# Moving the residual stream and the norms of a two-layer decoder trunk from feature order to token order, under a scheduler that looks ahead

## The chip, the cores and the metric

The kernel runs on the 8 cores of one Trainium2 chip. Every core works through one sequence of the batch on its own, without talking to the others. The metric is device time in microseconds (us) of the slowest core. Engines are called PE (the tensor engine), ACT (scalar), DVE (vector), POOL (GpSimd) and SP (sync).

Executions fall in two states. In the slow one, a die's cores are granted a lower PE clock and the run is some per cent longer, whatever the kernel.

## The reference, cut to what matters

```python
def rms_norm(x, g):
    y = x * lax.rsqrt(jnp.mean(x * x, axis=-1, keepdims=True) + 1e-6)
    return y * g

for layer in range(2):            # x is (8, 4096, 1024) float32
    h = h + 0.5 * rms_norm(swiglu(rms_norm(h, g0), wg, wu, wd), g1)   # hidden width 2816
    h = h + rms_norm(mixer(rms_norm(h, g2)), g3)   # layer 0: RG-LRU, layer 1: window attention
    h = h + 0.5 * rms_norm(swiglu(rms_norm(h, g4), wg2, wu2, wd2), g5)
```

There are six sub-layers, each with a norm before it and a norm after it. The mean of squares runs over the 1024 features of a token.

## The kernel before

A core cuts its 4096 tokens into 8 tiles of 512. Two tiles ("chains" 0 and 1) are always in flight, so that PE can multiply for one while the other is in a norm. The whole program is recorded as a graph of operations. A small list scheduler with a model of durations then fixes the order of the instructions on each engine. PE's order is fixed: an instruction whose input is late holds up everything behind it. Weights (float32 in memory) stream through slots in on-chip memory, and a DMA that POOL issues casts them to bf16.

Before the change the residual X lies in feature order: 128 features on the partitions, 512 tokens along the free axis, 8 chunks. The sum over features therefore crosses partitions, and PE does it, by multiplying the squares with a matrix of ones:

```python
X = [sb(f"X{s}", [128, NCH, T], F32) for s in range(NS_)]      # feature order, NCH = 8, T = 512

def norm_stats(s, src, key):                 # sum of squares over partitions, on PE
    h = Ps(s)
    for lo, hi in ((0, 6), (6, 8)):
        mm(s, [h], group(h, [ONES[:, :]] * (hi - lo), [src[s][:, kc, :] for kc in range(lo, hi)], ...
    return h

def rstd(s, h, to_psum):                     # x ** -0.5 as exp(-0.5 * ln(x)): an ACT table load
    act(s, ... out=RT[s][:, :], in_=PS[h.bank], func=AF.Ln, bias=EPSC[:, 0:1], scale=1.0 / D ...)
    act(s, ... out=PS[h.bank], in_=RT[s][:, :], func=AF.Exp, scale=-0.5 ...)

def norm_in(s, gcol):                        # the norm in front of a sub-layer
    ...                                      # squares, unless norm_out has made them
    h = norm_stats(s, SQ, "SQ")
    rstd(s, h, True)
    for kc in range(NCH):                    # PE may go on after the last of these
        dve(s, ... scalar_tensor_tensor(out=XN[s][:, kc, :], in0=X[s][:, kc, :],
            scalar=PV[:, gcol + kc:gcol + kc + 1], in1=PS[h.bank], op0=ALU.mult, op1=ALU.mult) ...)

def norm_out(s, gt, gcol, presq, final=None):   # norm after it, and the residual
    h = norm_stats(s, SQ, "SQ")
    rstd(s, h, True)
    ...                                      # 8 x (multiply, multiply-add) on DVE, squares on ACT
```

In the scheduler, each chain offers only the first operation of its queue on an engine:

```python
for q in qs:
    if q:
        o = q[0]
        r = self.ready(o)
```

Attention begins, after its norm, with two large memsets on DVE, which will matter later:

```python
dve(s, lambda e: e.memset(QZ[64:128, :, 0, :], 0.0), [], rQZ, n=4096)
dve(s, lambda e: e.memset(QZ[0:64, :, 1, :], 0.0), [], rQZ, n=4096)
```

## Time and profile before

| | before |
|---|---|
| time, median of 3 runs | 5182.59 us (5176.87 to 6037.99) |
| profiled run, slowest core | 5150.3 us, PE clock 0.977 |
| PE busy | 4786.3 us, 93% |
| PE idle before and between its instructions (sum over the timeline) | 335 us |
| rest of the span (after the last matmul, and gaps too short to be listed) | 29 us |

From the page of the kernel before: the engines' busy time, three rows of the span in 40 slices (busy share in tenths; PEclk is the granted clock in tenths) and the two large DMA queues (packets, MB, share of time).

```profile
PE 4786.3 (93%) x23872; PEld 2238.6 (43%) x23872; DVE 1951.0 (38%) x3805; ACT 2540.8 (49%) x4635; POOL 805.9 (16%) x1488
PE   6989899998999898999999989899899998999868
PEclk9989999999999999999999999999999999999989
DMA  8979778996999885999689978699698997869927
q0 software_dynamic: 213120, 666.99, 81.3%
q1 hardware_dynamic: 18720, 33.74, 2.3%
```

PE is the limit, with holes, and the DMA row is not far below it: most slices stand at 8 or 9.

The groups of instructions that make the norm's sums and its root (busy us, mean ns | idle before them):

```profile
L316 PE MATMUL psall<-SQ,ONES 128*128 128x512 bf16 x720 | 192.7, 402 | 127.9 <-ACT SQ L440 80.8 <-ACT SQ L403 44.3 <-ACT SQ L529 2.1
L509 ACT ACT_TABLE_LOAD x127 | 162.9, 1283 | 104.9 <-PE psall L316 102.7 <-DVE XN L409 1.1
L391 ACT ACT_TABLE_LOAD x82 | 105.2, 1283 | 65.7 <-PE psall L316 65.0
```

The mean of 402 ns is the length of one matmul's record, and such records overlap. Back to back one takes 0.216 us (94 matmuls in 20.45 us at 1599.83 in PE's timeline).

What PE waits for (total us, times, longest):

```profile
PE psall L316 <- ACT SQ L440: 80.8, 8, 12.2
PE psall L316 <- ACT SQ L403: 44.3, 3, 34.8
PE psall L316 <- ACT ST L743: 40.5, 84, 0.6
PE psall L775 <- ACT FB L781: 36.0, 72, 0.5
PE psall L316 <- DVE XN L409: 29.6, 5, 7.2
PE psall L316 <- DMA W<-wgu: 25.4, 9, 5.4
PE psall L316 <- DVE HST L635: 25.4, 3, 8.5
```

Eight waits of up to 12 us stand for the squares of an input norm, and a few of 7 to 8.5 us follow them. One such place in PE's timeline (start, us, instruction, count, idle before it):

```profile
1772.07 2.08 PE L316 MATMUL psall<-SQ,ONES 128*128 128x512 bf16 x8
1786.34 3.50 PE L316 MATMUL psall<-SQ,ONES 128*128 128x512 bf16 x8 [12.19 <-ACT SQ L440]
1798.30 3.57 PE L316 MATMUL psall<-XN,W 128*128 128x512 bf16 x8 [8.47 <-DVE HST L635]
```

The first row sums the output norm, the second the next input norm. PE sits idle 12.2 us while residual and squares are made, and 8.5 us while root and multiplies are made. (The profile names HST L635 for the second wait because that small copy ended last on DVE, at 1798.17. The last of the eight multiplies that PE needs ended 0.1 us before it.) The other tile is in its recurrence and has nothing for PE.

The rows also show a second cost of such gaps. Eight ones-matmuls take 2.08 us before the gap and 3.50 us after it, because the granted clock has fallen:

```profile
1780.00:1790.00 10.00, 3.50 (x8) 1.02 (x8) 10.00 (x17) 5.82 (x11) 0.00 (x0) 0.52 0.38 77
```

(The columns are those of the next table; the clock is 0.52.) In this trace the clock stands at 0.5 in 24 stretches of 3.4 to 24 us. Worked out from these records, the PE work inside them took some 55 us longer than at full clock.

The last 300 us in windows of 50 us (PE busy; PEld; DVE; ACT; POOL; clock; DMA share; GB/s):

```profile
4900.00:4950.00 50.00, 35.96 (x321) 24.52 (x319) 35.54 (x116) 44.72 (x142) 2.64 (x5) 0.97 0.33 54
4950.00:5000.00 50.00, 31.51 (x217) 18.46 (x214) 20.89 (x65) 35.85 (x92) 2.11 (x4) 0.81 0.31 60
5000.00:5050.00 50.00, 40.57 (x168) 17.36 (x169) 14.84 (x23) 11.06 (x17) 4.75 (x9) 0.85 0.59 112
...
sum 300.00, PE 220.44 PEld 110.44 DVE 104.57 ACT 124.38 POOL 32.61; mean PE 36.74 PEld 18.41 DVE 17.43 ACT 20.73 POOL 5.43
```

One tile is left alone here, with its attention and its last FFN, and PE is busy 220 of 300 us. In the trace the last attentions of the two tiles begin 431 us apart (at 4489 and 4920).

### The profile page before, as it was taken

How to read it: one execution, taken by the hardware profiler on the slowest of the kernel's cores; microseconds unless marked ns; L12 is line 12 of the kernel's file. 1: busy time of each engine (PE TensorE's matmuls, PEld its weight loads, DVE VectorE, ACT ScalarE, POOL GpSimd, SP SyncE). 2: the span in 40 equal slices, each digit the busy share in tenths (PEclk: the TensorE clock that was granted, in tenths of full speed). 3: DMA queues.
4: the chain of work that ended last, by engine and by line, in shares of the span. 5: the costliest groups of instructions: out<-in, count | busy, mean ns of one | idle time of the engine just before them, and what ended most of it. 6: DMA issues, size and time to landing. Idle time of an engine off the chain costs nothing.

```text
span 5150.3 us, 71937 instructions; the slowest of 8 cores (5110.8 to 5150.3 us)
## 1 busy us (share of the span) xinstructions
PE 4786.3 (93%) x23872; PEld 2238.6 (43%) x23872; DVE 1951.0 (38%) x3805; ACT 2540.8 (49%) x4635; POOL 805.9 (16%) x1488
## 2 busy tenths in 40 slices
PE   6989899998999898999999989899899998999868
PEld 2434344444444344444444434444444443444333
DVE  1344353225352426324444343521534344432251
ACT  2466365227563637424565463732747365453261
POOL 1111111210121110121112111012111211111101
PEclk9989999999999999999999999999999999999989
DMA  8979778996999885999689978699698997869927
GB/s 135 151 113 146 120 119 154 148 161 110 153 149 155 126 134 100 176 147 148 126 135 166 153 119 146 110 152 158 105 172 135 162 146 125 137 113 147 154 54 119
DMA packets 232200, 705.33 MB, mean 137 GB/s; under 512 B 25760, under 2 KB 26016, under 8 KB 231840
## 3 DMA queue, kind: packets, MB, share of 16 engines
q0 software_dynamic: 213120, 666.99, 81.3%
q1 hardware_dynamic: 18720, 33.74, 2.3%
q8 instruction: 201, 3.29, 0.3%
q14 instruction: 159, 1.30, 0.1%
HBM read 1317.19 MB, written 33.55 MB: 262 GB/s over the span
## 4 chain that ended last, share of the span: by engine, by line
PE 81%; ACT 6%; DVE 4%; DMA 4%; issue 3%; SPq 0%; POOL 0%; DVEq 0%; ACTq 0%; POOLq 0%
PE psall L316 81%; DMA W<-wgu 4%; ACT FB L736 2%; DVE ST L727 1%; ACT FB L781 1%; DVE XN L409 1%; DVE FB L758 1%; DMA X<-xT 1%; DVE FB L419 1%; PE psall L775 0%; ACT ST L743 0%; DVE ST L751 0%; ACT L391 0%; ACT RT L391 0%; ACT psall L394 0%
## 5 line engine op out<-in xcount | busy, mean ns | idle before, releaser
L316 PE MATMUL psall<-XN,W 128*128 128x512 bf16 x12864 | 2836.5, 381 | 85.4 <-DVE XN L409 29.6
L316 PEld LDWEIGHTS psall<-XN,W 128*128 128x128 bf16 x12864 | 1261.2, 98 | 1620.0 <-issue 134.3
L511 DVE TENSOR_TENSOR BIG<-SG,psall 128x512 bf16<-128x512 bf16 x704 | 478.4, 686 | 2166.4 <-PE psall L316 2075.5
L316 PE MATMUL psall<-BIG,W 128*128 128x512 bf16 x5632 | 1223.6, 379 | 0.0
L509 ACT ACTIVATE SG<-psall 128x512 bf16<-128x512 f32 x704 | 418.9, 597 | 1118.8 <-PE psall L316 1047.6
L316 PEld LDWEIGHTS psall<-BIG,W 128*128 128x128 bf16 x5632 | 551.0, 98 | 664.5
L870 POOL DMA_DIRECT2D W<-wgu x704 | 385.8, 549 | 2481.9 <-PE psall L316 2127.4
L527 ACT ACTIVATE FB<-psall 128x512 f32<-128x512 f32 x256 | 152.3, 595 | 818.8 <-PE psall L316 818.8
L870 POOL DMA_DIRECT2D W<-wdn x512 | 270.2, 528 | 1212.4 <-PE psall L316 1174.3
L316 PE MATMUL psall<-SQ,ONES 128*128 128x512 bf16 x720 | 192.7, 402 | 127.9 <-ACT SQ L440 80.8
L419 DVE TENSOR_TENSOR FB<-FB,psall 128x512 f32<-128x512 f32 x320 | 215.1, 683 | 153.0 <-ACT psall L394 153.0
L440 ACT ACTIVATE SQ<-X 128x512 bf16<-128x512 f32 x320 | 200.7, 628 | 134.6 <-DVE X L435 129.6
L736 ACT ACTIVATE FB<-psall,ST 128x256 bf16<-128x256 f32 x512 | 260.6, 575 | 3.2 <-DVE ST L730 3.1
L409 DVE SCALAR_TENSOR_TENSOR XN<-X,PV,psall 128x512 bf16<-128x512 f32 x336 | 227.2, 742 | 87.9 <-ACT psall L394 87.8
L316 PE MATMUL psall<-HY,W 128*128 128x512 bf16 x1024 | 231.0, 387 | 5.1 <-DVE HY L638 4.4
L509 ACT ACT_TABLE_LOAD x127 | 162.9, 1283 | 104.9 <-PE psall L316 102.7
L727 DVE TENSOR_REDUCE ST<-psall 128x1 f32<-128x512 f32 x256 | 176.0, 688 | 71.7 <-PE psall L316 66.6
L870 POOL DMA_DIRECT2D W<-wmix x200 | 105.5, 528 | 603.0 <-PE psall L316 599.2
L625 DVE TENSOR_TENSOR FB<-FB 128x512 f32<-128x512 f32 x64 | 43.4, 690 | 344.3 <-ACT FB L621 344.0
L316 PE MATMUL psall<-BIG 128*128 128x256 bf16 x512 | 122.8, 272 | 51.4 <-ACT ST L743 40.5
L316 PEld LDWEIGHTS psall<-SQ,ONES 128*128 128x128 bf16 x720 | 71.5, 102 | 227.1 <-issue 153.9
L316 PEld LDWEIGHTS psall<-HY,W 128*128 128x128 bf16 x1024 | 102.0, 100 | 132.6 <-issue 17.0
(92 smaller groups left out, 3337.3 us busy)
## 6 DMA issues: line engine op xcount, KB each, us to landing
W<-wgu POOLq DMA_DIRECT2D x704, 512.0 KB, 8.0
W<-wdn POOLq DMA_DIRECT2D x512, 352.0 KB, 6.3
W<-wmix POOLq DMA_DIRECT2D x168, 512.0 KB, 8.0
X<-xT SPq DMA_DIRECT2D x64, 256.0 KB, 15.2
outT<-X SPq DMA_DIRECT2D x64, 256.0 KB, 8.4
outT<-FB POOLq DMA_DIRECT2D x64, 256.0 KB, 17.7
W<-wmix POOLq DMA_DIRECT2D x32, 256.0 KB, 5.6
PV<-pvec SPq DMA_DIRECT2D x1, 104.0 KB, 2.3
```

The source lines that it names most:

```text
L316: ins = e.matmul(out() if callable(out) else out, lhsT=lhs() if callable(lhs) else lhs, rhs=rhs() if callable(rhs) else rhs, start=st, sto ...
L409: dve(s, lambda e, kc=kc: e.scalar_tensor_tensor(out=XN[s][:, kc, :], in0=X[s][:, kc, :], scalar=PV[:, gcol + kc:gcol + kc + 1], in1=PS[h. ...
L419: dve(s, lambda e: e.tensor_tensor(out=FB[s][:, i, :], in0=FB[s][:, i, :], in1=PS[h.bank], op=ALU.mult), [("FB", s, i), h], [("FB", s, i)] ...
L440: act(s, lambda e, i=i: e.activation(out=SQ[s][:, i, :], in_=X[s][:, i, :], func=AF.Square), [("X", s, i)], [("SQ", s, i)], ps_in=False)
L509: act(s, lambda e, g=g, hg=hg: e.activation(out=SG[s][:, g, :], in_=PS[hg.bank], func=AF.Silu), [hg], [("SG", s, g)], tab="silu", ps=[hg])
L511: dve(s, lambda e, g=g, j=j, hu=hu: e.tensor_tensor(out=A[:, j, :], in0=SG[s][:, g, :], in1=PS[hu.bank], op=ALU.mult), [("SG", s, g), hu], ...
L527: act(s, lambda e, i=i, h=h: e.activation(out=FB[s][:, i, :], in_=PS[h.bank], func=AF.Copy), [h], [("FB", s, i)], ps=[h])
L727: dve(s, lambda e, h=h, mxc=mxc: e.tensor_reduce(out=ST[s][:, kk, mxc:mxc + 1], in_=PS[h.bank], axis=AX.X, op=ALU.max), [h], [("ST", s, kk ...
L736: act(s, lambda e, h=h, hf=hf, hh=hh, ngc=ngc: e.activation(out=EEs[kk][:, hh, :], in_=PS[h.bank][:, hf * 256:(hf + 1) * 256], func=AF.Exp ...
L758: dve(s, lambda e, hh=hh: e.tensor_scalar(out=EEs[kk][:, hh, :], in0=EEs[kk][:, hh, :], scalar1=ST[s][:, kk, 10 + hh:11 + hh], scalar2=Non ...
L781: act(s, lambda e: e.activation(out=PTs[kk], in_=ptb().rearrange("p (a q) -> p a q", a=8), func=AF.Copy), [h], [rPT[kk]], n=1024, ps=[h])
L870: return e.dma_start(out=W[:, p.slot, 0:ncols], in_=ap[:, 0:ncols])
```

## The change

The residual and the norms go to token order: 128 tokens on the partitions, 1024 features along the free axis, 4 blocks per tile. Then a sum of squares is what ACT's accumulator gives while it squares. The root is one number per token, which POOL makes by a power, and no table load is needed. The normed block goes back to feature order for the projections by 8 PE transposes. The down and output projections take the activations as the stationary operand, so their result comes out in token order. The gains of the norms now vary along the free axis and must be loaded as rows of 128 x 1024 float32 (512 KB each). The scheduler also gets lookahead: it may pick any of the next 10 operations of a chain on ACT and DVE, of the next 4 on POOL. Core of the diff, with cuts:

```diff
+WINDOW = {"act": 10, "dve": 10, "pool": 4}
...
-                    if q:
-                        o = q[0]
+                    for n_, o in enumerate(q):
+                        if n_ >= self.window.get(e, 1):
+                            break
                         r = self.ready(o)
...
-        X = [sb(f"X{s}", [128, NCH, T], F32) for s in range(NS_)]
+        X = [sb(f"X{s}", [128, 4, D], F32) for s in range(NS_)]
+        XT = [sb(f"XT{s}", [128, 2, D], BF16) for s in range(NS_)]
+        GR = [sb(f"GR{s}", [128, D], F32) for s in range(NS_)]       # and GB, GI
...
-        def norm_stats(s, src, key):
+        def rsqrt(s, o, i, add):
+            ...
+                pool(s, lambda e: e.tensor_scalar(out=NS[s][:, i:i + 1], in0=NS[s][:, i:i + 1], scalar1=add,
+                                                  scalar2=None, op0=ALU.add), ...)
+            pool(s, lambda e: e.tensor_tensor(out=NS[s][:, o:o + 1], in0=NS[s][:, i:i + 1], in1=NHALF[:, :],
+                                              op=ALU.pow), ...)
+        def norm_a(s, b):
+            act(s, lambda e: e.activation(out=XT[s][:, b % 2, :], in_=X[s][:, b, :], func=AF.Square, scale=1.0 / 32,
+                                          accum_out=NS[s][:, 16 + b:17 + b]), ...)
+            rsqrt(s, 20 + b, 16 + b, EPS)
+            dve(s, lambda e: e.scalar_tensor_tensor(out=XT[s][:, b % 2, :], in0=X[s][:, b, :],
+                                                    scalar=NS[s][:, 20 + b:21 + b], in1=GI[s][:, :],
+                                                    op0=ALU.mult, op1=ALU.mult), ...)
+        def norm_b(s, b):
+                for c in range(NCH):
+                    ins = e.transpose(PS[h.bank].bitcast(BF16)[:, c * 128:(c + 1) * 128],
+                                      XT[s][:, b % 2, c * 128:(c + 1) * 128], IDENT[:, :])
+            act(s, lambda e: e.activation(out=XN[s][:, :, b * 128:(b + 1) * 128], ..., func=AF.Copy), ...)
...
+        def load_row(s, which, r):
+                dma(s, "sp", gsem[which][s], (GR, GB, GI)[which][s][:, :], rows[r], ...)
...  # down projection, one of 4 blocks x 2 halves
+                            s, [hb[b]], group(hb[b], [A[:, f, b * 128:(b + 1) * 128] for f in range(lo, hi)],
+                                              [wcol(pcs[u // 4], u % 4 * 512, 512) for u in us], ...
```

## The prediction

> **What bounds it now.** The tensor engine (PE): the page's first part shows it busy 4786 of 5150 us (93%), ACT 49%, DVE 38%; the chain of waits is 81% PE. In the timeline 176 matmuls of 512 columns take 38.15 us, 0.216 us each, and 8 transposes of 128 columns 0.44 us, 0.055 each; the Trainium skill ("TensorE: Matmul & The Clock Gate", "Wait — 56ns, not 53.3ns?") gives 215.7 and 55.6 ns warm, and the trace agrees. The granted clock is 1.00 in busy stretches, about 0.9 in slices with gaps. PE idles 336 us in the timeline: 51 until the first projection, four places where both token tiles are in a norm at once (about 21 each), about 80 in the last 300 us, where one tile runs alone, short waits in attention, 25 for weights; 19 us more after PE's last matmul.
>
> A second limit is close: an FFN matmul needs 32 KB of new weights per 0.216 us, 152 GB/s, and the windows view shows DMA shares of 0.95 to 1.05 at 145 to 165 GB/s in FFN stretches, 0.6 in attention.
>
> **What changes.**
> - PE: the 768 ones-matmuls that sum squares go (166 us at 0.216). 1536 transposes come (1536 x 0.055 = 85 us). Projections keep number and width. Net -81 us, all on the critical path.
> - Exposed norms: before, the last matmul to the next projection goes through copy, square, ones-matmuls, Ln and Exp with a table load, 8 x (multiply + add) on DVE (11.4 us), squares, ones-matmuls, Ln and Exp, 8 multiplies (6 us). After, four 128-token blocks are pipelined; I estimate 14 us from ACT 3.4 us and DVE 3.1 us per block (worked out from 0.6, 0.63, 1.13, 0.68, 0.75 us in the trace), against about 24. PE's new order interleaves transposes with the other tile's matmuls. With the slow clock after each gap: about -50 to -80 us; start and end about -10.
> - ACT: norm Ln/Exp leave, and with them 82 table loads and many silu reloads, 1.28 us each (127 in all; skill "ScalarE: Activation LUTs", "What ACT_TABLE_LOAD costs", about 1283 ns; agrees). ACT near 2300 us, DVE near 2000: no limits.
> - POOL gets 896 tiny operations for the reciprocal roots in the in-order stream that issues weight DMAs: each can delay the other.
> - DMA: 112 row loads of 512 KB. At the 285 GB/s that the hardware queue's 33.7 MB in 2.3% imply, an estimate of 1.84 us each, 206 us of DMA time, some 3.7 us per FFN. With a faster PE, FFN stretches become DMA-limited: I expect weight waits of 25 us to grow to 60 to 100, giving gain back.
>
> **Sum.** PE busy about 4690, idle and ends about 310: span near 5000, time 5040 us, -2.7%. Range 4955 to 5130. Faster 0.68, within 2% 0.27, slower 0.05.
>
> **What would show it.** Ones-matmuls gone; transposes of the normed tile x1536, mean start-to-start 55 ns; PE busy 4660 to 4730; table loads halved; gaps of 12 + 8 us gone or below 10; PE waits for weights doubled or more; clock in busy stretches still 1.00.
>
> **What would make it wrong.** POOL's operations much slower than the 0.1 to 0.5 us of its present small ones, or stuck behind weight DMAs that wait for slots, so that PE, in fixed order, waits at transposes. Four weight slots held through attention. Or DMA having more room than I read, so that weight waits don't grow (below 4990).

## The result, and the profile after

| | before | after |
|---|---|---|
| median | 5179.73 us (4 runs) | 4955.77 us (4 runs) |
| fast runs | 5151.17, 5176.87, 5182.59 | 4949.39, 4951.37, 4960.18 |
| ratio of fast runs | | 0.9581, 95% interval 0.9528 to 0.9634 |
| span of the profiled run | 5150.3 | 4959.1 |
| PE busy | 4786.3 | 4684.0 |
| PE idle in the timeline | 335 | 254 |
| rest of the span | 29 | 21 |

Each kernel also had one slow run (6037.99 and 5499.92 us). A ratio is the mean time of one kernel's fast runs over that of the other's of the same rounds, so not quite the ratio of the medians. The result is correct. The change saves 4.2%, where 2.7% was predicted. Part of the 4.2% is chance: two of the three fast runs of before here (5176.87 and 5182.59) lie above the 5140 to 5146 us that it mostly took later. Against those the saving is 3.5 to 3.8% for the runs above, and 4.0% for a_again below.

The page after, same rows as before:

```profile
PE 4684.0 (94%) x24640; PEld 2247.2 (45%) x24640; DVE 2000.6 (40%) x3580; ACT 2237.9 (45%) x4396; POOL 1235.2 (25%) x2224
PE   6999999998999999999899999999989999999998
PEclk9999999999999999999999999999999999999999
DMA  9999995969999999596999999959699999995989
q0 software_dynamic: 190080, 666.98, 84.9%
q1 hardware_dynamic: 25632, 92.47, 6.0%
```

The holes in PE's row and the drop at its end are gone, and the DMA row is now at 9 nearly everywhere. q1 carries 59 MB more: the gain rows.

The groups that took the place of ones-matmuls, Ln and Exp:

```profile
L420 PE MATMUL psall<-IDENT,XT 128*128 128x128 bf16 x1536 | 119.4, 223 | 116.1 <-DVE XT L408 105.5 <-ACT HY L561 5.7 <-DVE BIG L724 3.4
L399 POOL TENSOR_TENSOR NS<-NS,NHALF 128x1 f32<-128x1 f32 x384 | 295.5, 772 | 45.5 <-POOL NS L397 8.6 <-ACT XN L425 0.8 <-ACT HY L561 0.8
L397 POOL TENSOR_SCALAR NS<-NS 128x1 f32<-128x1 f32 x256 | 121.3, 474 | 361.4 <-ACT BIG L508 260.4 <-ACT XT L404 86.7
L538 ACT ACT_TABLE_LOAD x81 | 103.9, 1283 | 4.6 <-PE psall L326 2.3
```

The 82 table loads of L391 are gone, and those for silu fell from 127 to 81.

PE's waits:

```profile
PE psall L420 <- DVE XT L408: 105.5, 62, 21.0
PE psall L326 <- DMA W<-wgu: 52.3, 29, 5.8
PE psall L326 <- DMA W<-wdn: 32.1, 14, 5.2
PE psall L326 <- ACT ST L801: 9.7, 19, 0.8
PE psall L833 <- ACT FB L839: 7.4, 14, 0.6
```

The 12 + 8 us pairs are gone. Some 60 waits for a normed block are left, mostly of about a microsecond; the longest, of 21.0 and 13.5 us, lie in the start. Weight waits, 25 us before, are 84 us in the two DMA rows together. A norm in the timeline after, between one tile's FFN and its next sub-layer:

```profile
1729.88 0.61 PE L420 MATMUL psall<-IDENT,XT 128*128 128x128 bf16 x8 [0.48 <-DVE XT L408]
1730.32 1.89 PE L326 MATMUL psall<-W,BIG 128*128 128x512 bf16 x8
...
1739.04 1.89 PE L326 MATMUL psall<-W,BIG 128*128 128x512 bf16 x8
1742.65 5.34 PE L326 MATMUL psall<-XN,W 128*128 128x512 bf16 x24 [1.72 <-ACT XN L425]
```

The transposes of one tile's blocks stand between 8-matmul pieces of the other's down projection. The waits shown are 0.5 and 1.7 us.

And the last 300 us:

```profile
4709.00:4759.00 50.00, 48.95 (x380) 29.69 (x379) 36.50 (x100) 44.68 (x122) 10.22 (x17) 1.00 0.44 67
4759.00:4809.00 50.00, 49.03 (x258) 23.32 (x257) 14.72 (x18) 12.67 (x24) 15.08 (x28) 1.00 1.01 187
4809.00:4859.00 50.00, 44.84 (x207) 19.98 (x205) 12.29 (x21) 8.13 (x17) 17.70 (x29) 0.99 1.04 157
...
sum 300.00, PE 272.44 PEld 136.19 DVE 105.89 ACT 119.43 POOL 67.03; mean PE 45.41 PEld 22.70 DVE 17.65 ACT 19.91 POOL 11.17
```

PE is busy 52 us more of the last 300, because the last attention now runs beside the other tile's FFN. The last attentions of the two tiles begin 194 us apart now (at 4492 and 4686), and 197 us apart in a_inorder below.

PE's idle time, added up from the timelines (by hand; weight waits inside the first and last stretch are counted there too, and the many short waits, some 110 us in each kernel and most of them in attention and norms, have no row of their own):

| idle of PE, us | before | after |
|---|---|---|
| first 65 us | 51 | 45 |
| waits for weights | 25 | 84 |
| gaps of 6 us or more between (count) | 87 (9) | 0 (0) |
| last 300 us | 61 | 12 |
| all | 335 | 254 |

### The profile page after: what moved, and what is told of

Same layout as the page of the kernel before. It is cut to its first block, busy times and chain, and to the rows that moved or that the text cites. A ratio compares the mean times of both kernels' runs of the same rounds, so it can differ in the third digit from the quotient of the medians.

```text
span 4959.1 us, 76408 instructions; the slowest of 8 cores (4922.2 to 4959.1 us)
## 1 busy us (share of the span) xinstructions
PE 4684.0 (94%) x24640; PEld 2247.2 (45%) x24640; DVE 2000.6 (40%) x3580; ACT 2237.9 (45%) x4396; POOL 1235.2 (25%) x2224
## 4 chain that ended last, share of the span: by engine, by line
PE 73%; DMA 9%; issue 5%; ACT 4%; DVE 4%; POOL 4%; POOLq 0%; SPq 0%; DVEq 0%; ACTq 0%
PE psall L326 71%; DMA W<-wgu 5%; DMA W<-wdn 3%; PE psall L420 2%; ACT XN L793 2%; POOL NS L399 2%; DVE XT L408 1%; POOL NS L397 1%; DMA X<-x 1%; POOL W L935 1%; DVE X L460 1%; DVE FB L566 1%; POOL NS L393 1%; ACT FB L839 0%; ACT HY L561 0%
## 5 line engine op out<-in xcount | busy, mean ns | idle before, releaser
L326 PE MATMUL psall<-W,BIG 128*128 128x512 bf16 x5632 | 1247.9, 382 | 32.4 <-DMA W<-wdn 32.1
L326 PEld LDWEIGHTS psall<-W,BIG 128*128 128x128 bf16 x5632 | 550.6, 98 | 697.2 <-issue 57.5
L566 DVE TENSOR_TENSOR FB<-psall,GR 128x512 f32<-128x512 f32 x240 | 155.7, 685 | 793.9 <-ACT HY L561 425.9
L408 DVE SCALAR_TENSOR_TENSOR XT<-X,NS,GI 128x1024 bf16<-128x1024 f32 x192 | 245.4, 1280 | 185.1 <-POOL NS L399 179.0
L399 POOL TENSOR_TENSOR NS<-NS,NHALF 128x1 f32<-128x1 f32 x384 | 295.5, 772 | 45.5 <-POOL NS L397 8.6
L425 ACT ACTIVATE XN<-psall 128x1024 bf16<-128x1024 bf16 x192 | 196.1, 1022 | 228.7 <-PE psall L420 228.3
L793 ACT ACTIVATE XN<-psall,ST 128x256 bf16<-128x256 f32 x512 | 244.1, 499 | 1.8 <-DVE ST L813 1.0
L326 PE MATMUL psall<-W,HY 128*128 128x512 bf16 x1024 | 234.0, 379 | 2.8 <-DVE XN L816 2.1
L460 DVE SCALAR_TENSOR_TENSOR X<-FB,NS,X 128x1024 f32<-128x1024 f32 x160 | 205.2, 1282 | 74.0 <-POOL NS L399 73.9
L404 ACT ACTIVATE XT<-X 128x1024 bf16<-128x1024 f32 x192 | 202.5, 1057 | 71.2 <-DVE X L460 34.1
L420 PE MATMUL psall<-IDENT,XT 128*128 128x128 bf16 x1536 | 119.4, 223 | 116.1 <-DVE XT L408 105.5
```

What stands on the lines that cost most here:

```text
L326: ins = e.matmul(out() if callable(out) else out, lhsT=lhs() if callable(lhs) else lhs, rhs=rhs() if callable(rhs) else rhs, start=st, sto ...
L399: pool(s, lambda e: e.tensor_tensor(out=NS[s][:, o:o + 1], in0=NS[s][:, i:i + 1], in1=NHALF[:, :], op=ALU.pow), [("NS", s, i), "NHALF"], [ ...
L404: act(s, lambda e: e.activation(out=XT[s][:, b % 2, :], in_=X[s][:, b, :], func=AF.Square, scale=1.0 / 32, accum_out=NS[s][:, 16 + b:17 + b]),
L408: dve(s, lambda e: e.scalar_tensor_tensor(out=XT[s][:, b % 2, :], in0=X[s][:, b, :], scalar=NS[s][:, 20 + b:21 + b], in1=GI[s][:, :], op0= ...
L420: ins = e.transpose(PS[h.bank].bitcast(BF16)[:, c * 128:(c + 1) * 128], XT[s][:, b % 2, c * 128:(c + 1) * 128], IDENT[:, :])
L425: act(s, lambda e: e.activation(out=XN[s][:, :, b * 128:(b + 1) * 128], in_=PS[h.bank].bitcast(BF16).rearrange("p (c q) -> p c q", c=NCH), ...
```

## The experiments

Two questions were put. Did the gain come from the token order, or from the scheduler's lookahead, which the prediction had not costed? Theory A says token order, rival B says lookahead. And what did the removed ones-matmuls, the added row loads and the added POOL steps each cost? The first four kernels ran on one chip, with the kernel before at 5140.37, 5145.92 and 5141.13 us. The next four ran on another chip (before, fast runs: 5143.84, 5145.54, 5177.04 and 5200.29), the last four on a third (before, fast: 5141.01 to 5173.58).

Even in a run that counts as fast, one die can be slowed a little: 5200.29 above has one die at a mean clock of 0.973, the other at 0.980. Where it matters I also give the slowest core of the dies that stayed at their kernel's full clock ("undisturbed"), slow runs' other die included. It is 5132 to 5147 us for before, 4946 to 4950 for the changed kernel (4959 in its profiled run) and 4928 to 4937 in a_again.

### b_window: the kernel before, with lookahead

```diff
+WINDOW = {"act": 10, "dve": 10, "pool": 4}
-                    if q:
-                        o = q[0]
+                    for n_, o in enumerate(q):
+                        if n_ >= self.window.get(e, 1): break
-            self.rd.setdefault(r, {})[(eng, chain)] = o
+            self.rd.setdefault(r, {})[(eng, chain) if eng in ("pe", "sp") else id(o)] = o
```

With it, operations of one engine that now stand close together in changed order got the waits that make them safe.

> The kernel before with only the change's scheduler: looking 10 operations ahead on ACT and DVE (4 on POOL), the exact reader tracking and the near-neighbour waits that it needs. Theory A (the gain is fewer PE passes plus a shorter, block-pipelined norm): within 1% of before, 5130 to 5200 us, double gaps of 12 and 8 us still there. Rival B (the gain comes from the better order of instructions): 5000 to 5080 us, the double gaps mostly gone.

Measured: correct; fast runs 5204.55 and 5213.35 us, ratio 1.0129 (1.0100 to 1.0159). Lookahead alone makes the old kernel slower by 1.3%. Rival B falls.

### a_inorder: the changed kernel without lookahead

```diff
-WINDOW = {"act": 10, "dve": 10, "pool": 4}
+WINDOW = {}
```

> The changed kernel with the lookahead taken out (queues in program order). Theory A: at most 1% slower than the changed kernel, 4955 to 5005 us. Rival B: most of the gain is lost, 5080 us or more.

Measured: correct; fast runs 5038.67, 5049.99 and 5067.04 us, ratio 0.9824 (0.9778 to 0.9869). The token order alone is worth 1.8%. PE's wait for a normed block here:

```profile
PE psall L420 <- DVE XT L408: 145.0, 77, 19.9
```

In its trace the gaps of 6 us and more are already gone and the last 300 us hold 18.5 us of idle time. So these two belong to the token order. But the full change measures 0.958 and 0.954 (on other chips, each against before on its own), 2.4 to 2.8 points less. These two ratios contain runs of before with a disturbed die. On undisturbed dies a_inorder takes 5037 to 5049 us, about 100 us under before, and the full change another 80 to 120 us less, so that lookahead adds about 2 points on top of the token order. The two were not run on one chip. Theory A, which allowed it 1%, missed. What it removes is short: PE's wait for the normed block is 145.0 us without lookahead and 105.5 with it, and all PE idle falls from 318 to 254 us although weight waits grow from 55 to 84.

So the same lookahead costs one layout 1.3% and gives the other about 2 points. The trace of b_window suggests why, and the last batch tests it.

### b_one: the kernel before with one ones-matmul per norm instead of 8 (wrong on purpose)

```diff
-            for lo, hi in ((0, 6), (6, 8)):
-                mm(s, [h], group(h, [ONES[:, :]] * (hi - lo), [src[s][:, kc, :] for kc in range(lo, hi)],
-                                 first=lo == 0, last=hi == NCH),
-                   [(key, s, kc) for kc in range(lo, hi)] + ["ONES"], [h], rem=-1.0)
+            mm(s, [h], group(h, [ONES[:, :]], [src[s][:, NCH - 1, :]]),
+               [(key, s, kc) for kc in range(NCH)] + ["ONES"], [h], rem=-1.0)
```

> The kernel before with one ones-matmul per norm where there were 8 (wrong result on purpose): 672 matmuls of 0.216 us go, 145 us. If PE passes count in full in the kernel before: 5020 to 5045 us. If another limit (weights by DMA) takes it up: 5080 us or more.

Measured: fast runs 5065.15 to 5092.15 us, ratio 0.9866 (0.9828 to 0.9904), about 70 us less. 672 matmuls went, worth 145 us at 0.216. PE busy fell by 156 us to 4630, but idle time rose from 335 to 406: the norm's chain still takes as long, and PE gets there sooner. About half of the removed PE work came back as waiting.

### a_ones: the changed kernel with 768 ones-matmuls put back, their result overwritten

```diff
             def fn(e):
                 ins = None
+                for c in range(4):
+                    e.matmul(PS[h.bank], lhsT=ONES[:, :], rhs=XT[s][:, b % 2, (c % 2) * 512:(c % 2) * 512 + 512],
+                             start=True, stop=True)
                 for c in range(NCH):
```

> The changed kernel with 768 ones-matmuls put back, four before each block's transposes (their results are overwritten, so the result stays right): 166 us of PE at 0.216 each. If PE passes count in full: 5110 to 5130 us. If stretches bound by weight DMAs (84 us of waits) hide some: 5060 to 5100 us.

Measured: correct; fast runs 5012.48, 5046.74 and 5051.35 us, ratio 0.9795 (0.9728 to 0.9862). That is 2.1 to 2.5 points above the changed kernel, or 110 to 130 us of 5143, but only 52 us between the profiled spans (5011.4 and 4959.1). The nominal cost is 166 us. The profiled spans are nearer the truth: two of the three fast runs have one die at 0.988, and undisturbed dies take 5003 to 5012 us, some 50 to 80 us above the changed kernel. Weight waits fall from 84 to 35 us and all idle from 254 to 168. Here too part of the PE work hides in waits that are there without it.

### a_again: the changed kernel once more, as the partner of the next three

> The changed kernel once more, as the measure for the three others on this chip: 0.958 of the kernel before, within 0.5%.

Measured: fast runs 4936.52, 4937.33 and 4937.64 us, ratio 0.9542 (0.9460 to 0.9623).

### a_norows: the gain rows loaded only once per buffer (wrong on purpose)

```diff
+        seen_rows = set()
         def load_row(s, which, r):
-            if r is not None:
+            if r is not None and (which, s) not in seen_rows:
+                seen_rows.add((which, s))
```

> The changed kernel without the reloads of gain and bias rows: only the first load into each of the 6 row tiles stays, 106 of 112 go (wrong result on purpose). If the 84 us of weight waits come from DMA bandwidth: waits of 25 to 40 us and a time 40 to 60 us below the changed kernel. Rival (the waits come from the order in which POOL issues, not from bandwidth): within 20 us of it.

Measured: 4864.70, 4866.28 and 4868.28 us, ratio 0.9405 (0.9325 to 0.9485): 71 us under a_again, more than expected. Queue 1 and the waits for weights in a_norows:

```profile
q1 hardware_dynamic: 10368, 36.88, 2.2%
PE psall L326 <- DMA W<-wgu: 14.4, 10, 4.8
```

and in a_again:

```profile
PE psall L326 <- DMA W<-wgu: 41.9, 21, 6.2
PE psall L326 <- DMA W<-wdn: 30.5, 11, 5.1
```

Without 106 of the 112 row loads, weight waits fall from 72 to 15 us, and the time by about as much. The grown weight waits were the row loads competing with the weight stream. The 57 us of waits are not all of the 71: PE busy also fell, from 4677.4 to 4660.5 us for the same 24640 matmuls, as fewer waits left fewer stretches at half clock.

### a_rows16 and a_rows16b: all 14 rows kept on chip in bf16, loaded once

```diff
-        GR = [sb(f"GR{s}", [128, D], F32) for s in range(NS_)]
-        GB = [sb(f"GB{s}", [128, D], F32) for s in range(NS_)]
-        GI = [sb(f"GI{s}", [128, D], F32) for s in range(NS_)]
+        ROW = sb("ROW", [128, 14, D], BF16)
...
+            (GR, GB, GI)[which][s] = ROW[:, r, :]
+            if r not in have:
+                have.add(r)
+                dma(s, "pool", gsem[r], ROW[:, r, :], rows[r], [], [("ROW", r)], 1 << 19)
```

Space for it came from dropping the six row buffers, the ones matrix and unused parameter columns.

> All 14 rows kept in bf16 and loaded once (right result within rounding; masks and constants packed tighter to make room). Same DMA saving as without reloads, so if bandwidth is the cause within 15 us of that run, 30 to 60 us below the changed kernel; otherwise within 20 us of the changed kernel.

> The resident-rows kernel once more, because its profile fell in the slow state: fast runs about 4870 to 4880 us, ratio to before about 0.945; in a fast profile weight waits of 15 to 20 us and PE idle under 200 us.

Measured: both correct. a_rows16: three fast runs of 4870.82, 4878.25 and 4911.21 us, ratio 0.9444 (0.9340 to 0.9549). a_rows16b: 4872.22, 4874.25 and 4897.33 us, ratio 0.9491 (0.9447 to 0.9535); in its profile weights cost 15 us and PE idles 190 us. The fast runs of a_rows16 lie 25 to 67 us under those of a_again on the same chip (the 25 us is the run of 4911.21, with one die at 0.988; the other two lie 58 to 67 us under), with right results: most of the cost of the row loads can be had back.

### a_noeps: the separate add of epsilon on POOL dropped (384 of 896 POOL operations)

```diff
-            else:
-                pool(s, lambda e: e.tensor_scalar(out=NS[s][:, i:i + 1], in0=NS[s][:, i:i + 1], scalar1=add,
-                                                  scalar2=None, op0=ALU.add), [("NS", s, i)], [("NS", s, i)])
...
-                        rsqrt(s, 12 + b, 4 + b, 8 + b)
+                        rsqrt(s, 12 + b, 4 + b, b)
```

> The small added constant under the roots left out (changes the result by less than rounding): 384 of 896 POOL operations go, 0.2 to 0.5 us each, and each norm's chain gets a step shorter. If POOL is off the critical path: 0 to 25 us below the changed kernel. If its steps hold up norms or weight DMAs: 50 us or more below.

Measured: within tolerance here, though it leaves out epsilon, so it is a test and not a version to keep; fast runs 4888.63, 4909.48 and 4918.04 us, ratio 0.9476 (0.9339 to 0.9613), 19 to 49 us under a_again. PE's wait for the normed block:

```profile
PE psall L417 <- DVE XT L405: 55.3, 39, 18.9
```

against 105.6 us in a_again. About 12 us of this difference are only a label: the gap at 47 us in the start is put down to XT in a_again (12.4 us) and to XN here (12.1 us). In time, the two slower fast runs have one die at 0.986 to 0.988; undisturbed dies take 4885 to 4897 us, about 40 us under a_again. POOL's small steps are in the chain that PE waits for. I did not get add and power into one instruction, so a version with epsilon and without the step was not run.

### b_window2 and b_winmem: why lookahead hurt the kernel before

DVE in b_window2 at a norm in front of attention (timeline of DVE):

```profile
684.38 3.47 DVE L669 MEMSET BIG<- 64x4096 bf16 x1 [0.91 <-issue]
688.84 3.47 DVE L670 MEMSET BIG<- 64x4096 bf16 x1 [0.98 <-ACT psall L398]
692.23 5.22 DVE L413 SCALAR_TENSOR_TENSOR XN<-X,PV,psall 128x512 bf16<-128x512 f32 x8
```

The memsets depend on nothing at that time, so the scheduler, looking ahead, fills DVE's wait for the root with them. The root is there at 688.54 (ACT L398, 687.94 and 0.60 us), just before the second memset begins, and the 8 multiplies that PE waits for, next in DVE's fixed order, start 3.7 us later. PE, in the same run:

```profile
697.71 3.57 PE L320 MATMUL psall<-XN,W 128*128 128x512 bf16 x8 [10.20 <-DVE XN L413]
```

Theory M: this is what cost b_window its 1.3%. b_window2 is b_window again. b_winmem makes the two memsets wait for the norm as well, by naming its last output among what they read:

```diff
-            dve(s, lambda e: e.memset(QZ[64:128, :, 0, :], 0.0), [], rQZ, n=4096)
-            dve(s, lambda e: e.memset(QZ[0:64, :, 1, :], 0.0), [], rQZ, n=4096)
+            dve(s, lambda e: e.memset(QZ[64:128, :, 0, :], 0.0), [("XN", s, 7)], rQZ, n=4096)
+            dve(s, lambda e: e.memset(QZ[0:64, :, 1, :], 0.0), [("XN", s, 7)], rQZ, n=4096)
```

> The kernel before with lookahead, unchanged, as the partner of b_winmem on the same chip: fast runs about 1.013 of before, as in the first batch; in the profile, PE waits on the vector engine's XN of about 120 us in all, with seven gaps of about 10 us.

> The same, but the two 3.47 us memsets of attention now also wait for the last XN of the norm, so they cannot run ahead of its multiplies. Theory M (lookahead hurt before because those memsets jumped ahead of a norm that PE was waiting for): the seven 10 us gaps go back to what they were without lookahead or below, PE's waits on XN fall by 50 us or more, and the time comes to 0.995 to 1.002 of before (about 50 to 90 us under b_window2). Rival (lookahead hurts by starting weight loads worse or by reordering generally): time stays within 20 us of b_window2, about 1.010 to 1.015 of before.

Measured: both correct. b_window2: fast runs 5214.77 to 5248.12 us, ratio 1.0165 (1.0118 to 1.0211). b_winmem: 5110.78, 5123.97, 5128.82 and 5130.33 us, ratio 0.9962 (0.9935 to 0.9989). PE's wait for XN, first b_window2, then b_winmem:

```profile
PE psall L320 <- DVE XN L413: 124.2, 15, 10.2
```

```profile
PE psall L320 <- DVE XN L413: 53.1, 8, 7.6
```

The 10.2 us gaps, seven before, are all gone (gaps of 6 us or more: 14 with 143 us, then 7 with 72 us), and so are about 100 us of time. The delay by the memset itself is 3.4 us of each 10.2 us gap; the rest of the gap, and the slow clock after it, went with it. Theory M holds. With the memsets held back, lookahead is worth 0.4% to the old layout, which still has its 12 + 7.5 us pairs and 59 us of idle in its last 300 us: lookahead could not take those away.

### a_best: resident rows, and the memsets held behind the norm

```diff
-            dve(s, lambda e: e.memset(QZ[64:128, :, 0, :], 0.0), [], rQZ, n=4096)
+            dve(s, lambda e: e.memset(QZ[64:128, :, 0, :], 0.0), [("XN", s, 3)], rQZ, n=4096)
...  # on top of a_rows16, and the same for the second memset
```

> Resident rows and the memsets held behind the norm. Theory M says less here, as the change's norms are cut in four blocks and the memset costs one gap of 3 us per tile at most: 10 to 25 us under a_rows16b. Rival: nothing, or slower, because the memsets now stand between the norm and the evictions of K, V and Q: 0 to +10 us.

Measured: correct; fast runs 4849.93, 4853.52, 4853.62 and 4900.34 us, ratio 0.9468 (0.9383 to 0.9552). Its median fast run lies 21 us under that of a_rows16b on the same chip. The two intervals overlap, and the run of 4900.34 does not show it, but that run has one die at 0.989. Undisturbed dies take 4848 to 4853 us in all five runs, against 4869 to 4875 in a_rows16b. In the traces, four waits of 3 us for a normed block (at 775, 2002, 3204 and 4404 us of a_rows16b) are gone. So the step is worth about 20 us. PE idles 181 us, at a mean clock of 0.997 to 0.998 on all cores. This version beats both kernels: 5.3% under the kernel before, and some 80 to 110 us under the changed one's fast runs on the other chips (one run apart).

## Why the prediction was right or wrong

The sum was PE busy 4690, plus idle and ends 310, plus 40 from the profiled span to the time, which makes 5040. Measured: 4684, plus 275, and a median 3 us below the profiled span, which makes 4956. Of the 84 us between the two, 6 belong to PE busy, 35 to idle time and 43 to the added 40. The measured 4956 is at the very edge of the range that I gave (4955 to 5130).

1. **PE busy: right in size.** Predicted 4660 to 4730, measured 4684. The ones-matmuls went and 1536 transposes came. Not all of the fall of 102 us is instructions, though: they account for 81 us, and the loss by work at half clock fell from 55 to 41 us. a_best runs the changed kernel's matrix work, 16 instructions more, in 4647 busy us at a clock of 0.998, against 0.989: 37 us less, and its loss at half clock is 36 us smaller. Of the marks that I had listed one missed: table loads fell by a third (337 to 226), not by half.
2. **"Net -81 us, all on the critical path": too strong.** b_one removed 145 us of PE work and gained 70. a_ones put 166 us back and lost some 50 to 80 on undisturbed dies. PE work removed from a kernel that also has waits was worth between a third and a half of its time here.
3. **Exposed norms, "about -50 to -80 us": the step that failed, by size.** The mechanism was right: blocks pipelined, 12 + 8 us pairs gone. But I took each exposed norm to shrink from about 24 to 14 us. The transposes of its blocks went between the other tile's matmuls instead, and nothing of 6 us or more stayed: 87 us became 0. And for the 80 us of idle time that I had listed in the last 300 us there was only the "start and end about -10". In the timeline these are 61 us, and they fell to 12. Together 136 us of idle time went, and 6 more in the first 65 us, where 60 to 90 were expected. a_inorder shows that both came with the token order: the two tiles now follow each other at half the distance (194 and 197 us between their last attentions, 431 before). Why the scheduler now keeps the two tiles so close was not isolated.
4. **Lookahead: not costed at all.** The prediction reads the change as a change of layout. a_inorder shows that without lookahead the kernel takes 5039 to 5067 us, just where I had put the whole change: a coincidence, since the 40 in my sum had no basis. About 2 points of the gain exist only with lookahead. Yet it is no gain of its own: on the old layout it was 1.3% slower, and 0.4% faster with the memsets held. The token order gives it short independent pieces to move, and that may be why the parts do not add up. This last reading fits the traces, where about 40 us of waits for the normed block vanish with lookahead, but no run varied the size of the pieces.
5. **Weight waits: right.** Predicted 60 to 100 us, measured 84; row loads estimated at 206 us of DMA time, measured about 179 (6.0% of 4959 less 2.3% of 5150). a_norows shows that the rows were the cause, and that they cost 71 us. I had taken a time below 4990 as a sign that the weight waits had not grown; they did grow, and the time was below it all the same.
6. **POOL: named as the danger, and partly so.** The power took 0.77 us on average and the add 0.47, where I had hoped for 0.1 to 0.5. a_noeps shows a cost of about 40 us, from some 40 us of waits. It did not stop the gain.
7. **The added 40 us: no basis.** The median of before had lain 32 us above its profiled span, because its fast runs spread from 5151 to 5183. I carried that over to a kernel whose runs lie on its span. Later fast runs of before were mostly 5140 to 5146, so the pad was chance, as is part of the measured 4.2%.

## What to carry to other kernels

Put a reduction where an engine's accumulator gives it in a pass that is made anyway, then cut the chain in blocks that can slip between another tile's matmuls; here the long exposed waits then vanished rather than shrank. Count a wait of PE twice: here the clock often stood at half after waits of 3 us and more. Cost every part of a change by itself, schedulers too: the one here helped the layout with short pieces by about 2% and the other by at most 0.4%, and it can run a long ready operation (here a 3.5 us memset) ahead of the one that the bottleneck waits for, which an extra dependency undoes. When DMA is near its limit, count every byte that a new layout reloads per tile, and keep what fits.

## What the Trainium skill lacked or had wrong

- "TensorE: Matmul & The Clock Gate", "Seeing it yourself": it says to budget 1.95 GHz, 13/16 of full clock, for sustained dense matmuls on all cores. All 8 cores here ran dense matmuls, PE was busy 91 to 96% of the profiled spans, and the fast runs were granted 0.969 to 0.998 on average. In the traces the figure appears as stretches at exactly 0.8125: 842 us on core 0 of a_rows16's slow profile, 156 to 162 us on single cores of a_noeps, a_rows16b and b_winmem, none in the profiles of before and after. Only slow runs came near it as a mean (down to 0.806 in one of before). So here it is a state that comes and goes, not a constant.
- "GPSIMD Engine Reference", "3.1 Elementwise — side-by-side cycle accounting": it times operations of 512 and 2048 elements and gives no number for the dispatch on GpSimd (another section has only "tens of cycles" for the call). A 128x1 add took 474 ns on average and the power of 128x1 772 ns, in a chain that PE waited for. A price for such tiny operations, and one for the power, is missing.
- "ScalarE: Activation LUTs", "What it computes": the accumulator output is mentioned without a cost. In the trace every such activation is followed by an instruction that reads the accumulator, with a mean of 188 to 232 ns after the change (307 ns in the kernel before).
- "VectorE: DVE Perf Modes", "Zero memsets can be issued as uint32 (trn2)": it says a memset takes one cycle per element, and its table gives 0.96 GHz, which would be 1.04 ns. The memsets here took 3472 ns for 4096 elements and 272 for 256, so 0.83 ns per further element. By its advice, zeros written as uint32 are half the elements, so by my estimate about half the time of the 3.47 us memsets that did the harm; no run here shows it.
- "DMA: Bandwidth & Descriptors", "Issuing engines are not separate DMA queues": it says that DMAs of all issuing engines run on the same 16 DMA engines and interleave. No page has a number for a plain load competing with a stream of casting weight loads: 59 MB more on the hardware queue cost 71 us here while the windows showed DMA shares of 1.01 to 1.04.
